# A second load that waits for the identity matrix: cross-entropy over 32,000 classes on one NeuronCore

## The chip, the core and the metric

The kernel runs on one core of a Trainium2 chip. The metric is the device time of one execution in microseconds (us); a time given for a kernel is the median of several executions. A profile is one further execution, recorded by the hardware profiler. Its span counts from the first to the last instruction of the core and is therefore a little shorter than the device time.

The engines have short names: PE is TensorE, DVE is VectorE, ACT is ScalarE, POOL is GpSimd, SP is SyncE. A q behind the name (SPq, ACTq) is the engine's queue of transfers that it issues. Sixteen DMA engines move the data.

## What is computed

For each of 256 rows of 32,000 float32 logits, the kernel gives the negative log-probability of the labelled class:

```python
def reference(logits, labels):            # logits (256, 32000) float32, labels (256,) int32
    batch = logits.shape[0]
    log_probs = logits - np.max(logits, axis=-1, keepdims=True)
    log_probs = log_probs - np.log(np.sum(np.exp(log_probs), axis=-1, keepdims=True))
    return np.array([-log_probs[i, labels[i]] for i in range(batch)]).astype(np.float32)
```

The kernel uses the equal form log(sum over c of exp(x[c]) * exp(-x[label])), without subtracting the maximum. So it needs every logit once (32.77 MB) and the labelled logits a second time, by a gather.

## The kernel before

The logits come in 14 loads, numbered from 0. Each fills all 128 partitions; the number of elements per partition is in `LOADS`. Load 0 is small (1024 per partition), so that ScalarE can begin early; load 1 is the largest (14976).

```python
GROUPS = [64, 128, 32, 32]
LOADS = [
    [1024, 14976],
    [8896, 8192, 8320, 6592],
    [4736, 3264],
    [2496, 1824, 1344, 992, 736, 608],
]
SLOTS = [0, 1, 2, 3, 4, 5, 2, 3]      # loads 6 and 7 reuse buffers 2 and 3, the tail reuses buffer 1
```

SyncE issues the loads. The first six wait for nothing; the others wait until a buffer is free:

```python
    def load(i):
        a = starts[i]
        nc.sync.dma_start(out=place[i], in_=flat[GROUP_OF[i]][:, a:a + CHUNKS[i]])      # L206
    ...
        first = len(set(SLOTS))
        for i in range(first):
            load(i)
        nc.scalar.dma_start(                                                            # L229
            out=words[:, :], in_=bass.AP(tensor=lbl_words, offset=0, ap=[[2 * B, 1], [1, 2 * B]])
        )
```

The labels (2 KB) go through ScalarE's queue. They are cast, spread over the partitions by two small matmuls, added to row offsets, and used by GpSimd for two gathers of the labelled logits. GpSimd also makes an identity matrix early on, with a fill and a select:

```python
        nc.vector.tensor_copy(out=lbl_row[:, :], in_=words[:, 0:2 * B:2])               # L237
        ...
        for r in range(ROWS):
            nc.gpsimd.iota(out=idx[:, r:r + 1], pattern=[[1, 1]], base=r * P * C, channel_multiplier=C)
        make_identity(nc, ident[:, :])                  # masks.py:197 (fill) and masks.py:199 (select)
        nc.gpsimd.tensor_add(out=idx[:, :], in0=idx[:, :], in1=lbl[:, :])
        for r in range(ROWS):
            nc.gpsimd.indirect_dma_start(out=g_at[:, r:r + 1], ...)                     # L250
```

For each chunk ScalarE takes the exponential in place (L215); VectorE sums most of the chunks (L294), ScalarE the others; TensorE adds up partial sums, weighted by exp(-x[label]) (L300). The exponential of the gathered logits stands behind chunk 1's on ScalarE, and the identity is first used after it:

```python
        def step(i):
            exps(i)
            ...
            if i == GATHERED:                           # GATHERED = 1
                nc.scalar.activation(out=eg[:, :], in_=g_at[:, :], func=AF.Exp, scale=-1.0)
                for r in range(ROWS):
                    nc.vector.tensor_scalar_mul(diag[r][:, :], ident[:, :], eg[:, r:r + 1])
                ...
```

Once the program is built, two functions rearrange it. The second takes the landing of the result out of the engines' closing steps. The first puts the issue of load 0 ahead of the barrier with which all engines begin:

```python
def begin_first_load_before_barrier(nc):
    main, body = nc.m.functions[0].blocks[:2]
    rest = list(body.instructions)
    first = next(i for i in rest if i.engine == mybir.EngineType.SP and i.opcode == "DMACopy")
    rest.remove(first)
    head = list(main.instructions)
    at = next(
        k for k, i in enumerate(head) if i.engine == mybir.EngineType.SP and i.opcode == "Drain"
    )
    head.insert(at, first)
    main.instructions = head
    body.instructions = rest
```

So load 0 is issued before the barrier, and loads 1 to 5 directly after it, one after the other.

## Time and profile before

| | us |
|---|---|
| device time, median of 3 executions | 82.84 (82.63 to 83.09) |
| span of the profiled execution | 81.5 |
| ScalarE busy | 57.4 (70% of the span) |
| VectorE busy | 27.6 (34%) |
| TensorE matmuls busy | 11.7 (14%) |
| GpSimd busy | 5.2 (6%) |
| bytes read | 32.77 MB, mean 402 GB/s over the span |

The profile's line of busy tenths shows the span in 40 equal slices of about 2 us: a digit 9 is a slice in which the unit was busy 90% or more. ScalarE and the DMA engines side by side:

```
ACT   6320000000299999999999992499969999999993
DMA   4999999569969799799699699999899999999910
```

The DMA engines are at work from the first slice to the last but one. ScalarE does a little at the start (chunk 0), waits for the long load 1, and works from 22 us on with few breaks.

In the profile's timeline each line has the start in us, the duration in us, the engine, the line of the kernel, the operation, what is written and read, and in brackets how long the engine had been idle and what released it. A line with SPq or ACTq is the issue of a transfer, not the transfer. The trace also records each DMA packet (start, duration, size) and each increment of a semaphore; a load adds 16 to its semaphore, one from each DMA engine, and has landed with the sixteenth.

### The profile page before, as it was taken

To read this page: it belongs to the slowest core of one execution; us is meant where nothing else is said; L and a number is where in the kernel's file an instruction comes from. 1 tells how busy PE (TensorE), PEld (TensorE's weight loads), DVE (VectorE), ACT (ScalarE), POOL (GpSimd) and SP (SyncE) were. 2 spreads that over 40 slices of the span, in tenths; PEclk is the share of its full clock that TensorE was granted. 3 is DMA by queue.
4 is the path that set the end of the run, shared out by engine and by line. 5 is a ranking of instruction groups with operands and counts; after the bars stand their busy time and mean duration, and the time that the engine had idled before them with its cause. 6 is when DMAs were issued, how large, how long until landed. Compare 5 with 4: busy or idle time off the path is not lost.

```text
span 81.5 us, 261 instructions
## 1 busy us (share of the span) xinstructions
PE 11.7 (14%) x66; PEld 6.5 (8%) x66; DVE 27.6 (34%) x28; ACT 57.4 (70%) x23; POOL 5.2 (6%) x20
## 2 busy tenths in 40 slices
PE   0004000000000000051000020020000200259971
PEld 0003000000000000040000000000000000035640
DVE  1010000000000000022019917940099289898870
ACT  6320000000299999999999992499969999999993
POOL 4003881000000000000000000000000000000000
DMA  4999999569969799799699699999899999999910
GB/s 84 645 471 441 471 471 441 235 294 471 542 297 542 332 507 468 322 499 499 290 507 507 294 507 459 414 427 414 360 446 446 408 436 409 409 430 415 409 74 1
DMA packets 2084, 32.77 MB, mean 402 GB/s; under 512 B 290, under 2 KB 291, under 8 KB 1060
## 3 DMA queue, kind: packets, MB, share of 16 engines
q1 hardware_dynamic: 2018, 32.77, 94.5%
q0 software_dynamic: 64, 0.00, 0.1%
q10 hardware_dynamic: 2, 0.00, 0.0%
HBM read 32.77 MB, written 0.00 MB: 402 GB/s over the span
## 4 chain that ended last, share of the span: by engine, by line
DMA 61%; ACT 33%; SPq 1%; another core or an unknown queue 1%; issue 1%; PE 0%
DMA x<-in_logits_dram 61%; ACT x L215 24%; ACT x_tail L215 9%; SPq L206 1%; PE bank L300 0%; ACT res L222 0%
## 5 line engine op out<-in xcount | busy, mean ns | idle before, releaser
L215 ACT ACTIVATE x<-x 128x1024 f32<-128x1024 f32 (+7 forms) x8 | 48.1, 6030 | 22.0 <-DMA x<-in_logits_dram 22.0
L294 DVE SCALAR_TENSOR_TENSOR x<-x 128x4448 f32<-128x4448 f32 (+5 forms) x6 | 21.8, 3631 | 15.3 <-ACT x L215 15.3
L276 DVE TENSOR_SCALAR diag<-ident,eg 128x128 f32<-128x128 f32 x2 | 0.5, 282 | 27.8 <-ACT eg L274 27.8
L300 PE MATMUL bank<-weights,near 128*1 128x32 f32 (+1 forms) x24 | 3.6, 263 | 33.4 <-DVE x L294 32.4
L215 ACT ACTIVATE x_tail<-x_tail 128x2496 f32<-128x2496 f32 (+5 forms) x6 | 7.4, 1303 | 0.0
L291 PE MATMUL bank<-diag,x 128*1 128x128 f32 x32 | 5.8, 370 | 0.0
L279 PE MATMUL bank<-diag,ones 128*128 128x128 f32 x4 | 1.2, 460 | 28.4 <-DVE diag L276 28.4
L294 DVE SCALAR_TENSOR_TENSOR x_tail<-x_tail 128x1248 f32<-128x1248 f32 (+3 forms) x4 | 4.1, 1026 | 0.6 <-ACT x_tail L215 0.3
L300 PEld LDWEIGHTS bank<-weights,near 128*1 128x1 f32 x24 | 1.0, 82 | 36.0 <-DVE x L294 34.7
L291 PEld LDWEIGHTS bank<-diag,x 128*1 128x1 f32 x32 | 3.5, 113 | 2.1
L279 PEld LDWEIGHTS bank<-diag,ones 128*128 128x128 f32 x4 | 0.9, 321 | 28.5 <-DVE diag L276 28.5
L250 POOL DMA_INDIRECT g_at<-in_logits_dram,idx x2 | 2.1, 1030 | 0.6 <-issue 0.3
L239 PE MATMUL bank<-one,lbl_row 1*128 1x1 f32 x4 | 1.0, 352 | 5.9 <-DVE lbl_row L237 5.9
L198 ACT ACT_TABLE_LOAD x1 | 1.3, 1283 | 0.8 <-PEq L335 0.8
L237 DVE CAST lbl_row<-words 1x256 f32<-1x256 int32 x1 | 0.3, 281 | 4.5 <-DMA words<-in_labels_dram 4.5
L239 PEld LDWEIGHTS bank<-one,lbl_row 1*128 1x128 f32 x4 | 0.9, 316 | 5.9 <-DVE lbl_row L237 5.9
L265 POOL TENSOR_SCALAR_AFFINE_SELECT holds<-holds 128x32 f32<-128x32 f32 (+2 forms) x4 | 1.0, 238 | 0.3
L261 POOL TENSOR_SCALAR_AFFINE_SELECT holds<-holds 128x32 f32<-128x32 f32 (+2 forms) x4 | 1.0, 239 | 0.1
L282 DVE TENSOR_TENSOR weights<-holds,bank 128x256 f32<-128x256 f32 x1 | 0.4, 421 | 1.2 <-PE bank L279 1.2
L222 ACT ACTIVATE res<-bank 1x64 f32<-1x64 f32 (+2 forms) x3 | 0.7, 220 | 0.1
L248 POOL TENSOR_TENSOR idx<-idx,lbl 128x2 int32<-128x2 int32 x1 | 0.2, 195 | 5.6 <-DVE lbl L242 5.6
L242 DVE CAST lbl<-bank 128x2 int32<-128x2 f32 x1 | 0.2, 159 | 1.1 <-PE bank L239 1.1
(18 smaller groups left out, 4.0 us busy)
## 6 DMA issues: line engine op xcount, KB each, us to landing
x<-in_logits_dram SPq DMA_DIRECT2D x1, 7488.0 KB, 21.2
x<-in_logits_dram SPq DMA_DIRECT2D x1, 4448.0 KB, 31.3
x<-in_logits_dram SPq DMA_DIRECT2D x1, 4160.0 KB, 49.8
x<-in_logits_dram SPq DMA_DIRECT2D x1, 4096.0 KB, 40.5
x<-in_logits_dram SPq DMA_DIRECT2D x1, 3296.0 KB, 57.1
x<-in_logits_dram SPq DMA_DIRECT2D x1, 2368.0 KB
x<-in_logits_dram SPq DMA_DIRECT2D x1, 1632.0 KB, 15.3
x_tail<-in_logits_dram SPq DMA_DIRECT2D x1, 1248.0 KB
```

What stands on the lines that cost most here:

```text
L198: nc.scalar.preload_act_table_set("natural_log_exp_and_others")
L206: nc.sync.dma_start(out=place[i], in_=flat[GROUP_OF[i]][:, a:a + CHUNKS[i]])
L215: nc.scalar.activation(out=place[i], in_=place[i], func=AF.Exp, accum_out=acc)
L222: nc.scalar.activation(out=res[0:1, rows], in_=sums, func=AF.Ln)
L239: nc.tensor.matmul(lbl_up[:, r:r + 1], lbl_row[:, r * P:(r + 1) * P], one[:, :], start=True, stop=True)
L250: nc.gpsimd.indirect_dma_start(out=g_at[:, r:r + 1], out_offset=None, in_=logits[:, :], in_offset=bass.IndirectOffsetOnAxis(ap=idx[:, r:r ...
L261: nc.gpsimd.affine_select(out=h, in_=h, pattern=[[-q, k]], base=0, channel_multiplier=1, compare_op=mybir.AluOpType.is_ge, fill=0.0,)
L265: nc.gpsimd.affine_select(out=h, in_=h, pattern=[[q, k]], base=q - 1, channel_multiplier=-1, compare_op=mybir.AluOpType.is_ge, fill=0.0,)
L279: nc.tensor.matmul(spread[:, r * P:(r + 1) * P], ones[:, :], diag[r][:, :], start=True, stop=True)
L291: nc.tensor.matmul(warm, col, diag[0][:, :], start=True, stop=True)
L294: nc.vector.scalar_tensor_tensor(out=place[i][:, 0:half], in0=place[i][:, 0:half], scalar=1.0, in1=place[i][:, half:CHUNKS[i]], op0=mybir. ...
L300: nc.tensor.matmul(lane[g], near[i][:, :], weigh(g), start=i == first_of[g], stop=i == last_of[g])
```

## The change

SyncE gets one more instruction, a wait ahead of its first issue behind the barrier, which is that of load 1. It waits for GpSimd's semaphore to reach the value that it has once GpSimd's first select is done, the one that makes the identity matrix. The value is counted from the built program: the updates of GpSimd's instructions up to and with that select. No other instruction moves; the order on every engine is the same.

The wait isn't needed for the results: load 1 does not use the identity. It is for timing alone: load 0, already under way, and the labels' load on ScalarE's queue have the start to themselves for longer, and load 1 is queued behind them.

## The prediction

> **What bounds the kernel now.** I read four views, in this order: the chain of work that ended last, in order of time; the timeline of the first 6 us and of single loads; the busy times of short stretches; and the records of the single DMA packets. The chain first:

> ```profile
> 0.80 0.33 SPq L206
> ...
> 2.12 49.80 DMA x<-in_logits_dram
> ...
> 51.94 7.14 ACT x L215
> 59.08 0.62 another core or an unknown queue
> ...
> 59.73 5.62 ACT x L215
> ...
> 65.39 3.83 ACT x L215
> ...
> 69.45 2.91 ACT x L215
> 72.36 7.45 ACT x_tail L215 x8
> ```

> The columns are start, length and what. I number the loads from 0 (load 0 is 512 KB, load 1 is 7,488 KB). From 2.1 to 51.9 us nothing but the stream of loads decides. Then ScalarE takes chunk 4, waits 0.62 us, takes chunk 5 and is never idle for long again. The 0.62 us is called an unknown queue, but ScalarE starts at 59.73 and the trace's semaphore events have load 5's last increment at 59.705: it is a load too. So the end lies about 20 us after load 5 has landed. Loads 6, 7 and 8 land at 65.31, 69.19 and 72.16, each 0.1 to 0.3 us before ScalarE takes its chunk. There is almost no slack anywhere in the second half: if the whole stream moves by d, early or late, the end moves by d. (An earlier stream is also paid in full: the 2.56 us that ScalarE waits before 51.94 leaves room.)

> So the question is what the change does to the start of the stream. The start, from the timeline:

> ```profile
> 0.00 0.40 SPq L206 DMA_DIRECT2D x<-in_logits_dram  x1
> ...
> 0.80 0.33 SPq L206 DMA_DIRECT2D x<-in_logits_dram  x1
> ...
> 0.83 0.50 ACTq L229 DMA_DIRECT2D words<-in_labels_dram  x1
> ...
> 1.32 0.29 POOL masks.py:199 TENSOR_SCALAR_AFFINE_SELECT ident<-ident 128x128 f32<-128x128 f32 x1
> 3.50 1.06 ACT L215 ACTIVATE x<-x 128x1024 f32<-128x1024 f32 x1 [1.42 <-DMA x<-in_logits_dram]
> ...
> 5.59 0.28 DVE L237 CAST lbl_row<-words 1x256 f32<-1x256 int32 x1 [4.49 <-DMA words<-in_labels_dram]
> ```

> Load 0 is issued at 0.00, load 1 at 0.80, the labels on ScalarE's queue at 0.83; the identity is finished at 1.32 + 0.29 = 1.61 us; the labels are in use only at 5.59.

> Now the packets. Each load has its own packet length (a partition's share: 4,096 bytes for load 0, 59,904 for load 1), so that the packet records, sorted by size, give each load's start. Load 0: first packets at 1.02 us, the last begins at 2.98. Load 1: 16 first packets, one for each DMA engine, at 2.73 to 3.14 us, each 5 ns after that engine's 4-byte completion packet of load 0. The busy times of short stretches say the same: the engines are already full with load 0 when load 1 is in the queue. The eighth column is the DMA share, the last GB/s:

> ```profile
> 2.40:2.60 0.20, 0.00 (x0) 0.00 (x0) 0.00 (x0) 0.00 (x0) 0.00 (x0) 1.00 1.00 410
> 2.80:3.00 0.20, 0.00 (x0) 0.00 (x0) 0.00 (x0) 0.00 (x0) 0.00 (x0) 1.00 5.51 2353
> ```

> Before 2.7 us the share is 1.00 at 410 GB/s, all of it load 0. The 5.51 is no error: a packet is booked whole in the stretch where it starts, and a 59,904-byte packet takes 2.21 us. So **load 1, issued at 0.80, does not move a byte before 2.73**, 1.93 us later. It waits for load 0, not for its issue.

> [...] load 1's 5 ns behind load 0, and the labels' 2,048-byte packet (2.93 us), whose 4-byte completion packet comes only at 5.23, one load-1 packet (2.21 us) later. [...] here load 0's issue ends at 0.40 and its first packet starts at 1.02, 0.62 us later. [...] ScalarE's issue of one 2 KB row lasts 0.50 us beside SyncE's 0.33 us for load 1, which began 0.03 us sooner. [...]

> **The change, part by part.** It removes no work and adds one wait on SyncE ahead of load 1, for GpSimd's semaphore at 4. The build says that the fill of the identity brings it to 3 and the select at 1.32 us to 4, so the wait ends with that select and nothing later.

> 1. The issue of load 1. The select ends at 1.61. A signal to a waiting engine takes about 0.08 us (the cast of the labels ends at 6.97 + 0.16 = 7.13, GpSimd goes on at 7.21). The wait instruction itself is small: SyncE's one other bare wait is listed with 17 ns. So load 1 is issued at about 1.61 + 0.08 + 0.02 = 1.71 instead of 0.80: **0.91 us later**.

> 2. Its first packet. Load 0 is the model, with the same 128 rows: from issue to first packets 1.02 us, and the 16 engines' first packets lie, as far as I can tell them from second ones, between 1.02 and about 1.45. Then load 1 is ready on the engines from 1.71 + 1.02 = 2.73 to 1.71 + 1.45 = 3.16 us. Before, the engines were free for it from 2.73 to 3.14. [...] I set like against like: about 2.73 against 2.73, 3.16 against 3.14. **Exposed: about 0.0 us, with 0.2 either way** for the span on GpSimd and the latency (the store at the end has 0.74 us from issue to packet, so load 0's 1.02 may be on the long side; that would be slack, and gain nothing).

> 3. The issues behind it. Loads 2 to 5 follow at 0.45 us each, so the last is issued at about 3.5 instead of 2.6 us. Load 2's first packet starts at 20.56: 17 us of slack. Load 6 is issued at 47.22, released by VectorE, and its packets start at 58.39. Cost 0.

> 4. The labels. ScalarE's issue at 0.83 is now alone, some 0.9 us ahead of load 1, and its completion need no longer sit behind a 2.21 us packet: I expect them at about 3.1 us instead of 5.56, and the two gathers on GpSimd up to 2.4 us sooner (7.70 becomes about 5.3). Their use is the small exponential at 34.66, behind chunk 1's exponential, and they landed by 21.3. Slack over 13 us: gain 0.

> 5. The slowest DMA engine. One of load 1's first packets, the very first (2.731 us), took 3.276 us where the others took about 2.22, and that engine stays behind for the whole run: load 5's last two increments come at 59.174 and 59.705. A load has landed when its last engine is done, so this one engine costs the chain 59.705 - 59.174 = 0.53 us. I do not know why that packet was slow. It is the packet whose start the change touches, so it may go, or come on another engine. I give it one chance in four to go: an expected gain of 0.25 x 0.53 = 0.13 us.

> Sum: 0.0 + 0 + 0 - 0.13, from 82.84, gives 82.7 us.

> **The rivals.**

> *The whole delay comes through.* If a 128-row load's way to its first packet were 1.9 us, as the 0.80 to 2.73 of load 1 reads without the packets, the stream would move by the full 0.91: 83.75 us, 1.1% slower. The chain as printed (issue of load 1, then of loads 2 and 3, then DMA) suggests this. Against it stand the 5 ns between load 0's completion packets and load 1's first ones, and load 0's own 1.02. Even this rival stays within 2%.

> *A partial gap.* If GpSimd's real end is 0.2 to 0.3 us after the reported one, [...] the engines idle for 0.2 to 0.4 us each: 83.0 to 83.25 us.

> *The start becomes cleaner.* With the labels ahead and no load-1 packets queued, load 0 may land a little sooner and the slow engine may vanish. For it: the slow packet, and the labels behind a long packet. Against it: load 0's packets run at 159 ns each, back to back, from about 1.9 us on, so that nothing is seen to slow them, and chunk 0's exponential is 1.06 us in a wait that lasts to 21.98 in any case. It would make 82.2 to 82.4 us.

> *The labels' path becomes the bound*: no. It has 13 us of slack and gets shorter.

> **Range and chances.** The three times before lie from 82.63 to 83.09, so a median may be off by 0.2 without any effect. The gain side ends with the slow engine gone, 82.84 - 0.53 = 82.3, less noise 0.1: 82.2. The loss side takes a partial gap of 0.3 and noise 0.15: 83.3. Predicted 82.7, range 82.2 to 83.3. Two per cent is 1.66 us. No mechanism above reaches it: 0.91 is the most that the delay can cost, and the start of the stream can give back no more than the gap before 2.7 us. Faster by over 2%: 0.02; within: 0.95; slower: 0.03.

> **What would show the steps right or wrong.** Step 1: load 1's issue at 1.65 to 1.8 us in the timeline. Step 2: load 1's first packets still at 2.7 to 3.2 us, without a gap behind load 0's completions; first packets at 3.4 or later would prove the first rival. Step 3: the later issues shifted alike, and no engine waiting for them. Step 4: the cast of the labels at about 3.2 us, the gathers at about 5.3, ScalarE's small exponential still behind chunk 1's. Step 5: the last increment of load 5 less than 0.2 us, or again about 0.5 us, behind the one before it; an end that moves by about this difference. The prediction is wrong if the end moves by over 0.5 us either way, above all if each packet of the stream has changed its duration, for which I see no reason.

## The result, and the profile after

The change makes the kernel slower: 84.03 us (four executions, 83.93 to 85.26) against 82.93 us (82.63 to 83.09) on the same chip, a ratio of 1.0133 with a 95% interval of 1.0094 to 1.0173. Times here are medians of all executions, while the ratios leave out those more than 1.5% above the fastest of the same kernel, such as the 85.26. A second comparison on another occasion, for which I expected 84.0 us, gave 84.09 against 82.60 us, 1.0183 (1.0170 to 1.0196). The prediction was 82.7 us with a range up to 83.3.

The chain of work that ended last in the changed kernel, in order of time (start, length, what):

```profile
1.64 0.33 SPq L229
...
2.96 49.75 DMA x<-in_logits_dram
...
52.73 7.14 ACT x L238
59.87 0.62 another core or an unknown queue
...
60.51 5.63 ACT x L238
...
73.15 7.46 ACT x_tail L238 x8
```

The second half has moved as a block, by 0.78 to 0.79 us at each of these points, without a new wait. That part of the prediction holds: a shift of the stream is a shift of the end. The timeline of the same kernel:

```profile
1.32 0.29 POOL masks.py:199 TENSOR_SCALAR_AFFINE_SELECT ident<-ident 128x128 f32<-128x128 f32 x1
...
3.22 0.28 DVE L260 CAST lbl_row<-words 1x256 f32<-1x256 int32 x1 [2.13 <-DMA words<-in_labels_dram]
...
5.34 1.12 POOL L273 DMA_INDIRECT g_at<-in_logits_dram,idx  x1 [0.30 <-POOL idx L271]
...
22.75 12.68 ACT L238 ACTIVATE x<-x 128x14976 f32<-128x14976 f32 x1 [18.21 <-DMA x<-in_logits_dram]
```

Labels and gathers are 2.4 us earlier, as expected, and nobody gains by it; chunk 1's exponential starts at 22.75 instead of 21.98, the line of the kernel before:

```profile
21.98 12.68 ACT L215 ACTIVATE x<-x 128x14976 f32<-128x14976 f32 x1 [17.33 <-DMA x<-in_logits_dram]
```

So the loss is complete when load 1 lands. The busy times of short stretches of the changed kernel (the last two columns are DMA share and GB/s) show a hole:

```profile
2.40:2.60 0.20, 0.00 (x0) 0.00 (x0) 0.00 (x0) 0.00 (x0) 0.00 (x0) 1.00 0.85 348
2.60:2.80 0.20, 0.00 (x0) 0.00 (x0) 0.00 (x0) 0.00 (x0) 0.00 (x0) 1.00 0.50 195
```

In the kernel before the first of these stretches was at 1.00, and in the second load 1 had begun (a packet is booked whole where it starts):

```profile
2.60:2.80 0.20, 0.00 (x0) 0.00 (x0) 0.00 (x0) 0.00 (x0) 0.00 (x0) 1.00 1.97 689
```

In the changed kernel load 0 runs out, and load 1 is not there. How late the last engines get it, the DMA view of the stretch from 3.3 to 5.0 us tells. In the kernel before no packet starts in it, for every engine is busy with its first packet of load 1:

```profile
DMA packets 0, 0.00 MB, mean 0 GB/s; under 512 B 0, under 2 KB 0, under 8 KB 0
```

In the changed kernel three engines begin load 1 only there:

```profile
DMA packets 3, 0.18 MB, mean 106 GB/s; under 512 B 0, under 2 KB 0, under 8 KB 0
```

The packet records give the account. All numbers are us, from one profile each; a mean is over the 16 engines, "late" is the mean time from the completion packet of load 0 to the first packet of load 1, and "moving" is the mean time from there to the completion packet of load 1 (8 packets on each engine).

| | load 0 done, mean | late | load 1's first packets start | first packets take (median) | moving | load 1 done, mean | last engine |
|---|---|---|---|---|---|---|---|
| before | 2.98 | 0.01 | 2.73 to 3.14 | 2.22 | 17.82 | 20.81 | 21.51 |
| changed | 2.75 | 0.51 | 2.82 to 4.59 | 2.74 | 18.29 | 21.54 | 22.33 |
| changed, second profile | 2.98 | 0.60 | 3.09 to 4.31 | 2.89 | 18.32 | 21.90 | 22.65 |

For the first two rows: load 0 is done 0.23 sooner, the engines idle 0.50 longer, the packets take 0.47 longer; together about +0.73, which is the difference of the means (21.54 - 20.81). The last engine, for which ScalarE waits, is 0.82 later, and the span grew from 81.5 to 82.3. The second packets take what they took before (medians of 2.21 and 2.23). The start of load 1 is the whole difference.

### The profile page after: what moved, and what is told of

Same layout as the page of the kernel before. It is cut to its first block, busy times and chain, and to the rows that moved or that the text cites. A ratio compares the mean times of both kernels' runs of the same rounds, so it can differ in the third digit from the quotient of the medians.

```text
span 82.3 us, 261 instructions
## 1 busy us (share of the span) xinstructions
PE 11.9 (14%) x66; PEld 6.6 (8%) x66; DVE 27.6 (34%) x28; ACT 57.4 (70%) x23; POOL 5.2 (6%) x20
## 4 chain that ended last, share of the span: by engine, by line
DMA 60%; ACT 33%; SPq 1%; issue 1%; another core or an unknown queue 1%; POOL 1%; PE 0%; POOLq 0%
DMA x<-in_logits_dram 60%; ACT x L238 24%; ACT x_tail L238 9%; SPq L229 1%; POOL ident masks.py:199 0%; PE bank L323 0%; ACT res L245 0%; POOL idx L267 0%; POOL ident masks.py:197 0%; POOLq L267 0%; POOLq L358 0%
## 5 line engine op out<-in xcount | busy, mean ns | idle before, releaser
L317 DVE DVE_READ_ACCUMULATOR x<-x 128x1 f32 x6 | 0.5, 82 | 0.0
```

Of the source, the lines that this page charges most:

```text
L317: nc.vector.scalar_tensor_tensor(out=place[i][:, 0:half], in0=place[i][:, 0:half], scalar=1.0, in1=place[i][:, half:CHUNKS[i]], op0=mybir. ...
```

## The experiments

Two main theories. **Restart**: load 1's way from its issue to the engines is longer than what is left of load 0; the queues run dry, the engines begin at unequal times, and their first packets after such a start are slow. It should vanish if load 0 is long enough. **Delay**: whatever lies ahead in the queue, a load issued later costs its delay. Three smaller rivals are the issues of loads 2 to 5 (now at the time when load 1 starts), the labels' transfer and gathers (now ahead of load 1), and load 0's traffic, which might lengthen load 1's way. All ratios are to the kernel before, run beside each kernel. The packet times are from one profile of each.

### A longer load 0

The edit, with and without the change's wait:

```diff
 LOADS = [
-    [1024, 14976],
+    [2048, 13952],      # or [3072, 12928], or [4096, 11904]
```

Expected of load 0 = 2048, without the wait and with it:

> Without the wait, load 0 doubled to 2048 elements per partition, load 1 cut to 13952. Control for the next run. Both theories: 82.6 to 82.9 us, as the kernel before; the bytes are the same and the engines stay fed.

> The changed kernel's wait, with load 0 doubled to 2048. Load 0 should drain at about 4.0 to 4.4 us instead of 3.0. Restart theory: most engines have load 1 in their queue by then (its first packets came 1.2 to 1.6 us after an issue at 1.64, the latest 2.95), so most of the cost goes: 82.7 to 83.2 us. Rival, that a later issue costs its delay whatever is queued ahead: 83.7 to 84.2 us as before.

Expected of 4096, without and with the wait:

> Without the wait, load 0 four times as long (4096), load 1 11904. Control for the next run: 82.6 to 82.9 us by both theories.

> The changed kernel's wait, with load 0 of 4096. Load 0 should drain at about 6 us, after even the latest engine of the changed kernel (4.6 us) would have load 1. Restart theory: no cost, within 0.2 us of the control. Rival, that a later issue costs its delay whatever is queued ahead: about 1 us above the control.

Expected of 3072 with the wait:

> The changed kernel's wait with load 0 of 3072 (drain at about 5.2 to 5.7 us), between 2048 (cost 1.3 us) and 4096 (no cost). Restart theory: the latest engine with load 0 of 2048 had load 1 at 5.4 us, so nearly all is hidden: 82.6 to 83.0 us.

| load 0 | wait | us | ratio (95% interval) | load 0 done | load 1's first packets start |
|---|---|---|---|---|---|
| 2048 | no | 82.62 | 0.9997 (0.9982 to 1.0012) | 3.98 to 4.55 | 3.98 to 4.55 |
| 2048 | yes | 83.93 | 1.0159 (1.0128 to 1.0191) | 4.07 to 4.56 | 4.11 to 5.41 |
| 3072 | yes | 82.65 | 1.0000 (0.9989 to 1.0011) | 5.35 to 5.89 | 5.36 to 5.90 |
| 4096 | no | 82.62 | 1.0000 (0.9986 to 1.0015) | 6.46 to 6.91 | 6.46 to 6.92 |
| 4096 | yes | 82.68 | 1.0010 (0.9997 to 1.0023) | 6.53 to 7.12 | 6.54 to 7.12 |

The same wait and the same issue at 1.64 us cost nothing once load 0 lasts past 5.3 us. The delay theory falls; restart stands in its main point, that load 1's lateness costs nothing as long as load 0 lasts. (There is no run of 3072 without the wait; the other two lengths without it are as fast as the kernel before.) Two lines of the chain of the kernel with load 0 of 4096 and the wait:

```profile
1.64 0.33 SPq L229
...
59.40 5.64 ACT x L238
```

The issue is as late as in the changed kernel, and chunk 5 starts at 59.40 instead of 60.51. But my number for 2048 was wrong: I had expected most of the cost to go (82.7 to 83.2), and it stayed at 83.93. Three engines still get load 1 only at 4.85, 5.12 and 5.41, that is 3.2 to 3.8 us after the issue; and the first packets, 2.06 us in the control, have a median of 2.49, also on engines that show no idle time ahead of them. The idle time is only 0.20 us on the mean, the moving 0.53 us longer than in the control (17.07 against 16.54). So most of this cost is slow packets, and these do not need a queue that has run dry: that part of the restart theory fails. From load 1's issue to load 0's end 3.7 us were enough here (5.35 - 1.64), while 2.9 (4.56 - 1.64) were not.

### A shorter load 0

```diff
-    [1024, 14976],
+    [512, 15488],
```

> Without the wait, load 0 halved to 512 per partition, load 1 15488. Control for the next run, and a measure of how soon load 1 is ready when it is issued at 0.80: load 0 should drain at about 2.1 to 2.4 us. If load 1 then follows without a gap, its way from issue to first packet is at most 1.4 us when issued at 0.80; if there is a gap, the kernel before was itself near the edge, 82.8 to 83.5 us.

> The changed kernel's wait with load 0 halved to 512. Restart theory (load 1 comes to queues that have run dry): less of load 1's way is hidden, so the cost over the control grows to 1.6 to 2.3 us, 84.3 to 85.0. Traffic theory (load 1's way is long because the issue falls into load 0's traffic): half the traffic, so the late engines vanish and the cost shrinks, at most 1.0 us, 83.6 or less.

Measured: 83.54 us without the wait, 1.0100 (1.0080 to 1.0119); 84.01 with it, 1.0174 (1.0161 to 1.0187). Without the wait load 0 is done at 1.88 to 2.35 us, load 1 issued at 0.80 follows at 1.89 to 2.74 with hardly a gap (0.08 on the mean), yet its first packets take 2.72 (median) instead of 2.29: the same slow start, at a cost of 0.9 us. So the kernel before, with load 0 of 1024, had just enough queued ahead. The cost of the wait over its control is 0.47 us; that is far from restart's 1.6 to 2.3. It is within the traffic theory's "at most 1.0", but only because the control had lost 0.9 already, and the rest of that theory is not met: 84.01 is above 83.6, and late engines (3.43, 3.69 and 3.89) did not vanish. I had taken an undisturbed control for granted in both. The pair also gives the latest start of load 1 after an issue at 1.64: 3.89 us with load 0 of 512, against 3.93 to 4.59 in four profiles with 1024 (the changed kernel's two and the two runs below with the same issue) and 5.41 with 2048.

### Following issues

The edits, in words:

```diff
     # in the changed kernel (first run), in the kernel before (second run):
+    # SyncE also waits ahead of load 2 until GpSimd's semaphore is at 14 (all its early work done)
```

> The changed kernel, and load 2 (with loads 3 to 5 behind it) also waits, until GpSimd has finished all its early work (about 10 us). Restart theory (the engines' queues run dry between load 0 and load 1, and a restart from idle is slow): as the changed kernel, 84.0 us, load 1's first packets still 2.6 to 3.2 us long, the last engine again well behind. Following-issues theory (the issues of loads 2 to 5 now lie where load 1 begins and disturb it): load 1's first packets back to about 2.2 us and no engine that begins at 4.6, so 83.2 to 83.5 us.

> The kernel before (load 1 at once), and only load 2 with those behind it waits until GpSimd has finished its early work (about 12.5 us). Restart theory: load 1 is queued behind load 0 as before, so 82.9 us. Following-issues theory: the one slow first packet of 3.28 us goes as well, and the end comes up to 0.5 us sooner, 82.4 us.

Measured: 84.32 us, 1.0186 (1.0150 to 1.0222), for the first (hold_after), and 82.65 us, 1.0004 (0.9986 to 1.0021), for the second (hold_before). With loads 2 to 5 out of the way (issued from 10.46 us on), the changed kernel still starts load 1 at 2.98 to 4.33 us and its first packets still take 2.3 to 3.3. Following issues aren't the cause. The second run also has its labels early (the cast at 3.30 us, the gathers at 5.42) without any cost, which speaks against the next rival. Its profile has no slow engine (load 5's last two increments at 59.034 and 59.048), but its time is that of the kernel before: the slow engine that I had seen there belongs to that execution.

### Labels late again

The edit, in words:

```diff
     # in the changed kernel
+    # ScalarE waits ahead of the labels' load until load 0 has landed (its semaphore at 16)
```

> The changed kernel, with the labels' load on ScalarE's queue held back until load 0 has landed (about 3.4 us), so that it no longer comes between load 0 and load 1 and the gathers are late again. Restart theory: 83.7 to 84.3 us, as the changed kernel. Labels-first theory (the labels' transfer and the earlier gathers disturb load 1): back to 82.6 to 82.9 us.

Measured (labels_late): 84.25 us, 1.0218 (1.0176 to 1.0260). The labels aren't the cause. No engine was later than 3.93 us here, but the first packets were slower (2.3 to 3.4); load 1 is done at 22.01 us on the mean, against 21.54 and 21.90 in the two profiles of the changed kernel.

### Other doses of delay

The edits, in words:

```diff
-    wait for GpSimd's semaphore at 4 (identity made)
+    at 3 (identity filled); at 5 (labels added); for VectorE's at 2 (ones filled);
+    or no wait, and load 1 issued ahead of the barrier, behind load 0
```

> The other direction: load 1 is issued before the barrier too, directly behind load 0, at about 0.45 us instead of 0.80. Restart theory: load 1 was already queued behind load 0, so nothing is gained, 82.6 us (perhaps the slow first packet of one engine goes, at most 0.5 us). Rival, that each tenth of an earlier issue is worth a tenth: 82.3 us.

> Load 1 waits for VectorE's fill of the ones matrix, at about 1.1 us: an issue 0.3 us later than before and shorter than the wait for GpSimd's fill (1.27), which cost more than the change's own (1.64). If the cost grew with the delay: about 83.0. If an issue that falls right behind the labels' issue is what hurts some engines: 84 to 85 us.

> Load 1 waits for the fill of the identity (about 1.25 us), not for the select: about half the delay of the change. Restart theory: cost falls faster than the delay, since at an issue near 1.3 most engines still have load 0 in hand; 83.1 to 83.5 us. Following-issues theory: the issues of loads 2 to 5 end at about 4.1 us instead of 4.6, a cost between the two kernels too, 83.3 to 83.6. It mainly gives the dose.

> The wait for the fill once more, for a second profile: do the same number of engines (six) begin load 1 at about 4.6 us while the other ten begin at about 3.1? If the lateness is tied to what the queues are doing at the time of the issue: again several engines at 4.5 to 4.9. If it is chance: another number, and a time between 83 and 85.5 us.

> Load 1 waits until GpSimd has added the labels to the offsets (about 5.05 us), long after load 0 has landed. It measures a start from idle by itself. Restart theory: load 1 begins 1.0 to 1.2 us after its issue on most engines, its first packets take about 2.7 us as in the changed kernel or longer, and the end moves by the delay: issue 3.4 us later than in the changed kernel, 87.3 to 87.5 us. Following-issues theory: the same end, for the issues of loads 2 to 5 follow as closely as in the changed kernel; no decision from this one, only the latency.

| load 1 issued at | label | us | ratio (95% interval) | load 1's first packets start |
|---|---|---|---|---|
| directly behind load 0's issue | load1_early | 82.81 | 1.0004 (0.9984 to 1.0024) | 2.92 to 3.50 |
| 0.80 | the kernel before | 82.6 | 1 | 2.73 to 3.14 |
| 1.12 | wait_ones | 85.0 | 1.0213 (1.0155 to 1.0271) | fifteen by 3.28, one at 4.92 |
| 1.27 | wait_fill | 85.13 | 1.0280 (1.0241 to 1.0318) | ten by 3.32, six at 4.55 to 4.88 |
| 1.64 | the changed kernel | 84.09 | 1.0183 (1.0170 to 1.0196) | 3.09 to 4.31 |
| 5.26 | wait_labels | 87.02 | 1.0511 (1.0470 to 1.0553) | 6.22 to 7.20 |

Earlier than 0.80 gains nothing (in load1_early all that stands behind the barrier comes 0.47 us later as well, the labels' issue at 1.30 instead of 0.83). Later is not a matter of dose: an issue 0.47 us later (wait_fill) costs 2.5 us, more than one 0.84 us later. Its DMA view from 4.0 to 5.0 us, in which the kernel before has no packet:

```profile
DMA packets 6, 0.36 MB, mean 359 GB/s; under 512 B 0, under 2 KB 0, under 8 KB 0
```

These are six engines' first packets of load 1, over 3.2 us after the issue and 1.2 us or more after load 0 was done everywhere (3.32). ScalarE waits for the last engine (in the changed kernel load 1's sixteenth increment came at 22.729 us, and chunk 1's exponential started at 22.75), and here a group of six begins 1.6 us behind the others (4.63 and 3.06 on the mean). In the second profile of the same kernel (84.93 us) four engines were late, at 4.39 to 5.10. The number changes, the delay recurs.

Late engines are not the whole loss of wait_fill. Load 1 is done 1.79 us later on the mean than in the kernel before, and only 0.62 of that is idle time; 1.13 is slower packets, and these are not the first ones alone. The ten engines that began in time start their second packets between 5.05 and 6.0 us, after the late six have begun. The DMA view of that stretch in wait_fill:

```profile
q1 hardware_dynamic: 10, 0.60, 193.5%
```

And from 4.9 to 5.4 us in the kernel before, where 15 engines start their second packets:

```profile
q1 hardware_dynamic: 15, 0.90, 415.8%
```

The columns are packets, MB, and their time as a share of 16 engines in the stretch: 1.935 x 16 x 0.95 / 10 = 2.94 us for a packet in wait_fill, 4.158 x 16 x 0.5 / 15 = 2.22 us before. In the changed kernel, on the other hand, the two engines that began last (3.85 and 4.59) had first packets of 2.22 us, and the other fourteen 2.60 to 3.24. So in these two profiles it is rather a slow stretch around the start of load 1 (in wait_fill it reaches into the second packets, begun at 5.05 to 6.0) than a property of a first packet. What makes it slow is not known.

The executions of wait_ones spread from 83.7 to 85.2, so that by the median of all six it is 2.9% above the kernel before, and its profile with one late engine is of a long one; I lean on wait_fill. The expectation for wait_fill (83.1 to 83.6) was missed by far; that for wait_ones foresaw the larger cost for an issue right behind the labels', but the labels' own part in it was not tried at these two issue times.

wait_labels measures the way from idle engines: first packets 0.96 to 1.94 us after the issue, and 2.25 to 3.18 long (median about 3.0) instead of 2.21. Its cost, 4.4 us, is close to the 4.46 us of delay, but not because the delay comes through whole: load 1 starts 3.54 us later on the mean than in the kernel before, and its packets take 0.56 us longer in all.

## Why the prediction was wrong

**The bound** was right: from the landing of load 5 on, the end follows the stream. Load 5 landed at 60.490 instead of 59.705, 0.79 us later, and the span grew by 0.8.

**Step 1** was right: 1.71 expected, 1.64 measured.

**Step 2 failed**, and with it the sum: "Exposed: about 0.0 us, with 0.2 either way". The 0.2 was an estimate, and no trace had shown its part for GpSimd's span. The step was mis-sized in one term and lacked another. The term: load 1's way from issue to first packet was taken from load 0, "between 1.02 and about 1.45". It was 1.18 to 2.95 us in the changed kernel and up to 3.8 with load 0 of 2048. Load 0 is no model (the records carry no engine's number, so that even setting early against early and late against late was an assumption): it is issued to engines that do nothing, while load 1's issue falls into load 0's traffic. Even from idle engines load 1's way was 0.96 to 1.94 (wait_labels). The term is worth 0.50 us on the mean of the engines. The missing term: load 1's first packets take 2.74 us (median) instead of 2.22, which makes up the 0.47 us of longer moving. The kernel before had shown the like: a 4,096-byte packet takes 0.159 us in load 0's steady part, but ten of its early ones took 0.6 to 1.0. I had read those records and used only their starts. A sign that I had set was wrong too: "first packets at 3.4 or later would prove the first rival". Three engines began later than 3.4, and yet the longer load 0 refutes that rival.

**Step 3** was right in cost: the later issues shifted (load 5's issue lasted 1.14 us, from 3.43 to 4.57, instead of 0.57), nobody waited for them, and hold_after shows that they do no harm. **Step 4** was right in each number: cast at 3.22, gathers from 5.34, gain 0; labels_late shows that their time does not matter. Its reason is not shown: in hold_before load 1 is issued at 0.80 as ever, and the cast comes at 3.30 all the same.

**Step 5** was wrong in direction. I had given the one slow engine a chance to go. By my own sign, less than 0.2 us between load 5's last two increments, it went: they are at 60.369 and 60.490. But the one before is at 59.870, so now two engines trail by 0.5 to 0.6 us instead of one. The sign was badly chosen. Nor is the slow engine a property of the kernel before: profiles of other kernels without the wait (hold_before, load1_early) have none, and load 5 lands there at 59.05 and 59.36. The profiled execution of the kernel before was a long one (83.12 us, where the second comparison has a median of 82.60), which fits the smaller loss between the two profiles (0.8 us) than in the second comparison (1.5).

**The rivals.** The partial gap foresaw idle engines, but for 0.2 to 0.4 us each, where the mean was 0.51 and the end is set by the last engine (load 1 done there at 22.33 us, on the mean at 21.54), and without the slower packets. Nor was a late end of GpSimd seen as its cause: load 1's issue began at 1.64 us, 0.03 after the end of the select in the timeline (1.32 + 0.29). The full delay (83.75) came nearer in number for the wrong reason. "0.91 is the most that the delay can cost" was refuted by wait_fill: 0.47 us of delay, 2.5 us of cost.

**What stays open.** Shown is what an issue of load 1 at 1.64 us cost over the same kernel without the wait: 1.3 us with load 0's end at 4.07 to 4.56 (83.93 against 82.62), and less than 0.1 with its end at 6.53 to 7.12 (82.68 against 82.62). Why its way to some engines takes 3 us and more when it is issued into load 0's traffic, why packets around its start are slow even where no idle time is seen, and why an issue at 1.27 is worse than one at 1.64, is not. The latest starts grow with load 0 (1.94 us after the issue from idle, 2.25 with 512, up to 2.95 with 1024, 3.77 with 2048), which fits traffic in the way but does not show it. The labels fit it in part: their 2 KB go through ScalarE's queue and are issued at 0.83 or 0.84 (load1_early and labels_late apart), and yet their packet starts the later the longer load 0 is, up to 3072: at 2.0 and 2.1 us with 512, at 2.7 to 3.1 with 1024, 4.2 with 2048, 5.3 with 3072, then 4.6 and 4.9 with 4096. The records don't show what happens between an issue and its first packet.

## What to carry to other kernels

Here load 1's wait behind load 0 was free where load 0 lasted to 5.35 us or longer after an issue at 1.64 (82.65 and 82.68 us), and it was not in the changed kernel, where the engines idled for 0.51 us on the mean (84.03). The way to the engines under traffic has to be measured, not taken from the first transfer of the program: load 0's was read as 1.02 to 1.45 us, load 1's was up to 2.95 in the changed kernel. Issue the next load early, or make the one ahead long enough: here an issue at 0.80 us, ahead of load 0's first packet at 1.02, was just enough with a load 0 of 512 KB (82.6 us) and not with 256 KB (83.54), and an issue at 1.64 us was enough with 1.5 MB (82.65) and not with 1 MB (83.93). Where all engines share a transfer, ask for the last engine's start, not for the mean: in the changed kernel they were 4.59 and 3.25 us.

## What the runs showed of the hardware

With the engines idle, load 1 (128 partitions) reached them 0.96 to 1.94 us after the issue (wait_labels); issued into a running load 0, up to 3.8 us after it (load0_2048_wait), unequally over the engines: from 1.18 to 2.95 us after it in the changed kernel. The labels' 2 KB, issued into load 1 at 3.60 us (labels_late), had their packet at 8.47. In the changed kernel fourteen of the sixteen first packets of load 1 took 2.60 to 3.24 us, where the later ones took 2.21; with load 0 of 512 (load0_512) the slowest took 3.48 instead of 2.29 (61,952 bytes). In wait_fill second packets were slow as well (2.94 instead of 2.22 us). No packet of 59,904 bytes took less than 2.21 us in any profile, so that no engine that began late was seen to make up for it by faster packets.
